# A two-layer decoder trunk on one NeuronCore: products of 258 columns in the short runs of the output projections, and gaps between the later heads' outputs

## The chip, the core and the metric

The kernel runs on one core of one Trainium2 chip. The core has TensorE (PE in the profile; its weight loads are shown apart as PEld), VectorE (DVE), ScalarE (ACT), GpSimd (POOL) and SyncE (SP, which here only starts DMAs). They run side by side and wait for one another through semaphores. The metric is the device time of one execution, in microseconds; lower is better. Three runs of the kernel before gave 556.93, 557.33 and 557.66, median 557.33.

## What is computed

Two layers over 256 tokens of width 1024, in float32. Layer 0 mixes tokens by latent attention, layer 1 by block attention, which at 256 tokens and a block of 256 is causal attention with a relative bias. Each has 8 heads of 128, and each mixer is followed by a squared-ReLU MLP of width 4096.

```python
for i in range(DEPTH):
    h = rms_norm(x, attn_norm[i])
    if i % N_MIXERS == 0:
        x = x + mla_mixer(h, ..., mla_w_o[j], cos, sin)
    else:
        x = x + moba_mixer(h, ..., moba_w_o[j], positions, rel_bias_table)
    h = rms_norm(x, mlp_norm[i])
    x = x + sq_relu_mlp(h, mlp_w_in[i], mlp_w_out[i])
# the last step of either mixer, with out of shape (B, H, S, 128):
out.transpose(0, 2, 1, 3).reshape(B, S, H * 128) @ w_o
```

The change lies in that last step, the output projection, and in one row of layer 1's value projection.

## The kernel before

**Products.** A float32 operand is kept as two parts, a high one rounded to PE's fp32r and the rest as a low one. A product of two such operands is made of three matrix products into the same PSUM bank: high by high, low weight by high activation, high weight by low activation (`mm3`, L87). In most of the program the weights stand still (128 x 128) and the activations move, 256 columns, one for each token. In layer 1's query, key and value rows it is the other way round: the activations of 128 tokens stand still and the weights move, 512 columns in two halves of 256 (`proj1_row`).

**Weights.** They come in units of 128 x 1024 floats. SyncE loads a unit (`load_one`, L158), ScalarE makes the high part (`hi`, L169), VectorE the low part (`lo`, L178). The calls `fill`, `both`, `hi` and `lo` in the program text set where that work stands in each engine's order.

**Order.** The pools are scheduled by hand: every engine runs its instructions in the order in which the program text issues them. So a product that waits holds up all that PE has to do after it.

**Heads.** `run_heads` works through the 8 heads of a layer. For each it issues logits (`A_`), weights of the softmax (`W_`), a transpose (`B_`) and the product with the values (`C_`, `values`, L600 to L606), which leaves the head's output, transposed, as 128 x 256: ScalarE writes the high part into `aT0`, VectorE the low part into `aT1`. Logits, transposes and values are plain float32 on PE. Between them stand short runs of the output projection, in fp32r products:

- `o(h)` adds head h's part to the first four of the eight output blocks; the accumulators `accs` are four PSUM banks. It is 4 x 3 = 12 products. Head 2 is cut into two runs of 6.
- `col(d, heads)` adds heads to one of the last four blocks. Block 4 is taken in pieces: heads 0 and 1 (6 products), 2 and 3 (6), 4 to 6 (9), and 7 (3). Blocks 5 to 7 are taken whole.

Head 6's `o`, the second half of block 4, head 7's `o`, blocks 5 to 7 and the start of the MLP follow each other with no plain float32 product between. That long run has 440 products in the trace, up to the sum of squares inside the MLP (`other_type`).

**Products of 258 columns.** `wider` (L103) makes one of the three products two columns wider than the 256. Its moving operand runs on into the first two columns of whatever lies behind, and its output into two columns of the bank that nobody reads. The third value names which of the three products it is. In the MLP one stands ahead of the first product group after each change of operand kind (the flag `moved`). In `col` there are two: at head 0 and at head 5 of block 4. A bank's columns 256 and 257 have to be written by the first product of the accumulation if a later one adds to them. In layer 1's rows, `proj1_row` with `wide` puts 258 columns in the seventh place and 254 in the last one, so that the row still has its 512; it does so for the first key row and the first query row.

**The heads' outputs.** `aT0` and `aT1` hold 8 x 256 columns each, the heads side by side, so the two columns behind head h are the first two of head h + 1.

Of the kernel before, what the change touches and what calls it, by code (L numbers as in the profile page):

```python
# [11 lines left out]
F32R = mybir.dt.float32r  # L12
# [6 lines left out]
P = 128  # L19


ROOM = {"hT": 416, "aT0": 0, "aT1": 224, "a0": 224, "a1": 224}
D = 1024
S = 256
NT = S // P
KD = D // P
H = 8
# [33 lines left out]
def trunk(ctx: ExitStack, tc: tile.TileContext, A, out):  # L61
    nc = tc.nc
# [8 lines left out]
    def ps():  # L71
        return psum.tile([P, 512], F32, name="ps", tag="ps")
# [14 lines left out]
    def mm3(o, a, b, start, stop, wide=None, between=None):  # L87

        for i, (w, t) in enumerate(((0, 0), (1, 0), (0, 1))):
            if wide and i == wide[2]:  # L90
                mm(wide[0], a[w], wide[1], start and i == 0, stop and i == 2)
            else:
                mm(o, a[w], b[t], start and i == 0, stop and i == 2)
            if between and between[0] == i:
                between[1]()
# [6 lines left out]

    def wider(bank, b, which=0):  # L103
        moved[0] = True
        return bank[:, :S + 2], flat(b[:, :2])[:, :S + 2], which

    def other_type(i, f):
        def run():
# [5 lines left out]
    def flat(ap):  # L114
        return ap.rearrange("p a b -> p (a b)")
# [86 lines left out]
    def part(u, sl):  # L202
        return u[0][:, sl], u[1][:, sl]
# [44 lines left out]
    mhalf = const.tile([P, 32], F32)  # L248
# [295 lines left out]
    def head_tiles(l):  # L544

        cm = ExitStack()
        pool = cm.enter_context(tc.tile_pool(name=f"heads{l}", bufs=1))
        r = []
        for c in range(2):
            r.append({n: pool.tile([P, *sh], F32, name=f"{n}{c}")  # L550
                      for n, sh in (("k", (HG, S)), ("q", (HG, S)), ("v", (NT, HG, P)))})
        room(pool, f"aT{l}")
        aT = [pool.tile([P, H, S], F32R, name=f"aT{i}") for i in range(2)]
        return cm, r, aT

    class Head:


        def __init__(self, hd, aT, h, bias, extra=None):
            self.aT = (aT[0][:, h], aT[1][:, h])  # L560
            self.two = [a[:, h:h + 2] for a in aT] if h < H - 1 else None
            self.i = h % HG
            self.hd = hd[h // HG]
            self.h, self.bias, self.extra = h, bias, extra
# [49 lines left out]
    def out_residual(a, d, gname):  # L614
        nc.vector.tensor_add(x[:, d], a, x[:, d])
        make_h_filled(d, gname)

    def run_heads(hs, proj, post, rows, turn, mid, base, gname, n1):
# [5 lines left out]
        accs = []  # L624

        def o(h, ds=range(4)):
            u = unit(base + h // 2)
            for d in ds:
                if h == 0:
                    accs.append(ps()[:, :S])  # L630
                c = (h % 2) * 512 + d * P
                mm3(accs[d], part(u, slice(c, c + P)), hs[h].aT, h == 0, h == H - 1)
                if h == H - 1:
                    out_residual(accs[d], d, gname)
            if h % 2:
                done(base + h // 2)

# [2 lines left out]
        def col(d, hh):  # L640
            if d not in late:
                late[d] = ps()
            u = unit(base + d)
            for h in hh:

                wide = None
                if d == 4 and h in (0, 5):
                    which = 2 if h and mid is not None else 0
                    wide = wider(late[d], hs[h].two[which // 2], which)
                mm3(late[d][:, :S], part(u, slice(h * P, (h + 1) * P)), hs[h].aT, h == 0, h == H - 1, wide)  # L650
            if hh[-1] == H - 1:
                done(base + d)
                out_residual(late[d][:, :S], d, gname)
# [189 lines left out]
    heads_ctx, hd, aT = head_tiles(0)  # L843
# [56 lines left out]
    post0("k1", 1, on_act=True)  # L900
    fill()

    run_heads([Head(hd, aT, h, bias0, (qpT, kpT)) for h in range(H)], proj0, post0, rows0, turn0, None, O0, "mlp0", 1)
    heads_ctx.close()
    mla_ctx.close()
# [191 lines left out]
    heads_ctx, hd1, aT1 = head_tiles(1)  # L1097
# [3 lines left out]
    def post1(name, t, root=True):  # L1101
        p = open_p.pop((name, t))
        if name[0] == "v":
            nc.scalar.activation(flat(hd1[int(name[1])]["v"][:, t]), p, AF.Copy, scale=r3[0][:, t:t + 1])
        else:
            norms[name, t] = Norm(p, P)
            if root:
                root1(name, t)
# [7 lines left out]
    def turn1(name, t):  # L1116
        tk = slice(t * P, (t + 1) * P)
        to_T(norms[name, t].y, hd1[int(name[1])][name[0]][:, :, tk], gqk[:, 1:2] if name[0] == "q" else None)
# [18 lines left out]

    def proj1(name, t, wide=False):
        open_p[name, t] = ps()
        for _ in proj1_row([(name, t, k, i, half) for k in range(KD) for i in range(3) for half in range(2)], wide):  # L1140
            pass
        if t == NT - 1:
            done(Q0 + 4 * order1[name] + 3)
# [35 lines left out]
    proj1("v0", 1)  # L1179
    fill(2)  # L1180
    post1("v0", 1)
    run_heads([Head(hd1, aT1, h, bias[:, h]) for h in range(H)], proj1, post1, rows1, turn1, lambda: turn1("q0", 1), O1, "mlp1", 2)
    heads_ctx.close()
    mlp(1, M1, [], {}, finish1)
# [74 lines left out]
```

## Time and profile before

| | us |
|---|---|
| runs shown | 556.93, 557.33, 557.66 |
| span of the profiled execution, first to last instruction | 556.0 |
| short runs and what lies between them, layer 0 | 61.0 to 81.6 |
| long run, layer 0 | 81.6 to 131.6 |
| second value row, layer 1 | 333.6 to 339.3 |
| short runs and what lies between them, layer 1 | 347.3 to 365.7 |
| long run, layer 1 | 365.7 to 415.7 |

The span runs from the first to the last instruction of one profiled execution; the time of a run also holds what lies around it, 1.3 us on the median. In rows of the timeline stand the start in us, the length in us, engine, line, operation, output and inputs by the program's names, the shapes, and the number of instructions merged in the row. `ps<-aT,wh` is a product of a head's output with the high part of a weight unit, `ps<-aT,wl` with the low part; `hTh` and `hTl` are the two parts of the normed activations, `pT` and `p` the softmax. In a row of the windows view, each engine's busy time stands with the number of its instructions in the window, then the granted clock, the share of the DMA engines and GB/s. Grouped rows end with count, busy us, mean ns of one, and the idle time before them.

### The profile page before, as it was taken

How to read it: one execution, taken by the hardware profiler on the slowest of the kernel's cores; microseconds unless marked ns; L12 is line 12 of the kernel's file. 1: busy time of each engine (PE TensorE's matmuls, PEld its weight loads, DVE VectorE, ACT ScalarE, POOL GpSimd, SP SyncE). 2: the span in 40 equal slices, each digit the busy share in tenths (PEclk: the TensorE clock that was granted, in tenths of full speed). 3: DMA queues.
4: the chain of work that ended last, by engine and by line, in shares of the span. 5: the costliest groups of instructions: out<-in, count | busy, mean ns of one | idle time of the engine just before them, and what ended most of it. 6: DMA issues, size and time to landing. Idle time of an engine off the chain costs nothing.

```text
span 556.0 us, 11405 instructions
## 1 busy us (share of the span) xinstructions
PE 550.4 (99%) x4648; PEld 538.5 (97%) x4648; DVE 394.4 (71%) x654; ACT 302.5 (54%) x495; POOL 90.6 (16%) x108
## 2 busy tenths in 40 slices
PE   9999999999999999999999999999999999999997
PEld 6888999999999999999999999999999999999997
DVE  5998777688997589965658366777867653977630
ACT  5899675674443364535464465746856432655420
POOL 4692100022132000012232100000130311000100
PEclk9999999999999999999999999999999999999999
DMA  8833534586567366545445554354866764565810
GB/s 294 300 108 128 163 117 152 190 279 191 183 202 220 117 219 195 171 173 186 156 153 195 168 169 145 121 190 121 268 221 184 234 192 148 184 211 175 275 40 28
DMA packets 29188, 99.60 MB, mean 179 GB/s; under 512 B 3824, under 2 KB 4720, under 8 KB 29136
## 3 DMA queue, kind: packets, MB, share of 16 engines
q1 hardware_dynamic: 28656, 97.94, 55.1%
q0 software_dynamic: 336, 0.92, 0.4%
q8 instruction: 36, 0.59, 0.4%
q14 instruction: 16, 0.13, 0.1%
q10 hardware_dynamic: 144, 0.02, 0.0%
HBM read 97.82 MB, written 1.05 MB: 178 GB/s over the span
## 4 chain that ended last, share of the span: by engine, by line
PE 94%; DMA 2%; DVE 1%; SPq 1%; POOL 1%; ACT 1%; issue 0%; ACTq 0%; DVEq 0%
PE ps L85 91%; DMA raw<-in_w_u 2%; PE ps L372 1%; PE ps L596 1%; DMA win<-in_w_in 1%; DVE wl L178 1%; POOL hrs L270 1%; ACT wh L169 0%; SPq L158 0%; PE ps L512 0%; SPq L230 0%; DVE t L352 0%; ACT sqj L477 0%; POOL rs L270 0%; SPq L235 0%
## 5 line engine op out<-in xcount | busy, mean ns | idle before, releaser
L178 DVE TENSOR_TENSOR wl<-raw,wh 128x1024 fp32r<-128x1024 f32 x177 | 218.2, 1249 | 34.9 <-ACT wh L169 34.4
L169 ACT CAST wh<-raw 128x1024 fp32r<-128x1024 f32 x177 | 182.4, 1046 | 69.4 <-PE ps L85 48.7
L85 PE MATMUL ps<-a,wh 128*128 128x256 f32 x1024 | 175.0, 276 | 0.0
L85 PEld LDWEIGHTS ps<-a,wh 128*128 128x128 f32 x1024 | 154.6, 188 | 0.0
L85 PE MATMUL ps<-hTl,wh 128*128 128x256 f32 x512 | 141.9, 277 | 0.0
L85 PE MATMUL ps<-a,wl 128*128 128x256 f32 x512 | 141.9, 277 | 0.0
L85 PE MATMUL ps<-hTh,wl 128*128 128x256 f32 x512 | 141.6, 277 | 0.0
L85 PE MATMUL ps<-hTh,wh 128*128 128x256 f32 x512 | 141.6, 276 | 0.0
L85 PEld LDWEIGHTS ps<-hTh,wh 128*128 128x128 f32 x512 | 96.2, 188 | 0.1
L85 PEld LDWEIGHTS ps<-hTl,wh 128*128 128x128 f32 x512 | 96.2, 188 | 0.1
L85 PEld LDWEIGHTS ps<-a,wl 128*128 128x128 f32 x512 | 96.2, 188 | 0.0
L85 PEld LDWEIGHTS ps<-hTh,wl 128*128 128x128 f32 x512 | 96.2, 188 | 0.0
L940 ACT ACTIVATE t<-ps 128x512 f32<-128x512 f32 (+1 forms) x34 | 19.4, 571 | 62.1 <-PE ps L85 62.1
L85 PE MATMUL ps<-aT,wh 128*128 128x256 f32 (+1 forms) x256 | 50.2, 288 | 0.0
L942 DVE SCALAR_TENSOR_TENSOR t<-ps,t 128x512 f32<-128x512 f32 (+1 forms) x34 | 22.4, 659 | 36.1 <-ACT t L940 35.8
L85 PE MATMUL ps<-wh,hTh 128*128 128x256 f32 (+2 forms) x224 | 45.7, 289 | 0.2 <-ACT wh L169 0.2
L85 PE MATMUL ps<-wh,hTl 128*128 128x256 f32 (+2 forms) x224 | 45.1, 284 | 0.5 <-DVE hTl L280 0.5
L85 PE MATMUL ps<-wl,hTh 128*128 128x256 f32 (+2 forms) x224 | 44.9, 285 | 0.4 <-DVE wl L178 0.3
L85 PEld LDWEIGHTS ps<-aT,wh 128*128 128x128 f32 x256 | 40.3, 188 | 0.2
L85 PE MATMUL ps<-aT,wl 128*128 128x256 f32 x128 | 35.7, 279 | 0.0
L85 PEld LDWEIGHTS ps<-wh,hTh 128*128 128x128 f32 x224 | 34.4, 189 | 1.1 <-issue 0.5
L85 PEld LDWEIGHTS ps<-wh,hTl 128*128 128x128 f32 x224 | 34.7, 188 | 0.8 <-DVE hTl L280 0.8
(167 smaller groups left out, 622.2 us busy)
## 6 DMA issues: line engine op xcount, KB each, us to landing
raw<-in_w_in_mlp SPq DMA_DIRECT2D x64, 512.0 KB, 4.3
raw<-in_w_out_mlp SPq DMA_DIRECT2D x64, 512.0 KB, 4.4
raw<-in_w_qkv SPq DMA_DIRECT2D x24, 512.0 KB, 4.2
raw<-in_w_u SPq DMA_DIRECT2D x8, 512.0 KB, 6.7
win<-in_w_in SPq DMA_DIRECT2D x8, 352.0 KB, 5.1
raw<-in_w_o0a SPq DMA_DIRECT2D x4, 512.0 KB, 3.6
raw<-in_w_o0b SPq DMA_DIRECT2D x4, 512.0 KB, 3.7
raw<-in_w_o1a SPq DMA_DIRECT2D x4, 512.0 KB, 4.2
```

Of the source, the lines that this page charges most:

```text
L85: nc.tensor.matmul(o, a, b, start=start, stop=stop)
L169: (eng.copy if eng is nc.scalar else eng.tensor_copy)(his[i][:, :w], raws[i][:, :w])
L178: eng.tensor_sub(los[i][:, :w], raws[i][:, :w], f32(his[i][:, :w]))
L270: nc.gpsimd.tensor_tensor(dst, t, mhalf[:, :n].rearrange("p (a b) -> p a b", b=t.shape[-1]) if len(t.shape) == 3 else mhalf[:, :n], op=OP.pow)
L372: nc.tensor.transpose(pt[:, i * P:(i + 1) * P], yf[:, i * P:(i + 1) * P], ident)
L596: nc.tensor.transpose(pt[:, i * P:(i + 1) * P], self.p[:, i * P:(i + 1) * P], ident)
L940: nc.scalar.activation(rl, src, AF.Relu)
L942: nc.vector.scalar_tensor_tensor(sq, src, 0.0, rl, op0=OP.max, op1=OP.mult)
```

## The change

- The heads' outputs get a new layout: flat, with 64 floats (256 bytes) between heads 4 and 5, 5 and 6, and 6 and 7. Heads 0 to 4 stay side by side. `fill_gaps` writes the first two columns of each gap, in both parts: one copy on GpSimd for `aT0` and one for `aT1`, ahead of `run_heads` in each layer.
- `o(h)`: head 0 takes 258 columns in the first product of output blocks 0, 1 and 2; heads 1, 2, 4, 5 and 6 in the third product of the first block of a run, so head 2 twice. Heads 3 and 7 stay as they are.
- `col(4, ...)`: head 2 takes 258 columns in its third product, beside heads 0 and 5 as before.
- Layer 1's second value row gets the 258 and the 254 that the first key row and the first query row have.

```diff
--- before.py
+++ after.py
@@ -19,6 +19,7 @@
 P = 128
 
 
+GAP = 64
 ROOM = {"hT": 416, "aT0": 0, "aT1": 224, "a0": 224, "a1": 224}
 D = 1024
 S = 256
@@ -102,7 +103,7 @@
 
     def wider(bank, b, which=0):
         moved[0] = True
-        return bank[:, :S + 2], flat(b[:, :2])[:, :S + 2], which
+        return bank[:, :S + 2], (b if len(b.shape) == 2 else flat(b[:, :2]))[:, :S + 2], which
 
     def other_type(i, f):
         def run():
@@ -550,15 +551,22 @@
             r.append({n: pool.tile([P, *sh], F32, name=f"{n}{c}")
                       for n, sh in (("k", (HG, S)), ("q", (HG, S)), ("v", (NT, HG, P)))})
         room(pool, f"aT{l}")
-        aT = [pool.tile([P, H, S], F32R, name=f"aT{i}") for i in range(2)]
+        aT = [pool.tile([P, H * S + 3 * GAP], F32R, name=f"aT{i}") for i in range(2)]
         return cm, r, aT
 
+    def fill_gaps(aT):
+
+        for a in aT:
+            nc.gpsimd.tensor_copy(a[:, 5 * S:].rearrange("p (a b) -> p a b", b=GAP + S)[:, :, :2],
+                                  mhalf[:, :6].rearrange("p (a b) -> p a b", b=2))
+
     class Head:
 
 
         def __init__(self, hd, aT, h, bias, extra=None):
-            self.aT = (aT[0][:, h], aT[1][:, h])
-            self.two = [a[:, h:h + 2] for a in aT] if h < H - 1 else None
+            c = h * S + max(h - 4, 0) * GAP
+            self.aT = (aT[0][:, c:c + S], aT[1][:, c:c + S])
+            self.two = [a[:, c:c + S + 2] for a in aT] if h < H - 1 else None
             self.i = h % HG
             self.hd = hd[h // HG]
             self.h, self.bias, self.extra = h, bias, extra
@@ -627,11 +635,16 @@
             u = unit(base + h // 2)
             for d in ds:
                 if h == 0:
-                    accs.append(ps()[:, :S])
+                    accs.append(ps())
                 c = (h % 2) * 512 + d * P
-                mm3(accs[d], part(u, slice(c, c + P)), hs[h].aT, h == 0, h == H - 1)
+                wide = None
+                if h == 0 and d < 3:
+                    wide = wider(accs[d], hs[h].two[0])
+                elif h not in (0, 3, H - 1) and d == ds[0]:
+                    wide = wider(accs[d], hs[h].two[1], 2)
+                mm3(accs[d][:, :S], part(u, slice(c, c + P)), hs[h].aT, h == 0, h == H - 1, wide)
                 if h == H - 1:
-                    out_residual(accs[d], d, gname)
+                    out_residual(accs[d][:, :S], d, gname)
             if h % 2:
                 done(base + h // 2)
 
@@ -644,8 +657,8 @@
             for h in hh:
 
                 wide = None
-                if d == 4 and h in (0, 5):
-                    which = 2 if h and mid is not None else 0
+                if d == 4 and h in (0, 2, 5):
+                    which = 2 if h == 2 or h and mid is not None else 0
                     wide = wider(late[d], hs[h].two[which // 2], which)
                 mm3(late[d][:, :S], part(u, slice(h * P, (h + 1) * P)), hs[h].aT, h == 0, h == H - 1, wide)
             if hh[-1] == H - 1:
@@ -900,6 +913,7 @@
     post0("k1", 1, on_act=True)
     fill()
 
+    fill_gaps(aT)
     run_heads([Head(hd, aT, h, bias0, (qpT, kpT)) for h in range(H)], proj0, post0, rows0, turn0, None, O0, "mlp0", 1)
     heads_ctx.close()
     mla_ctx.close()
@@ -1137,6 +1151,7 @@
 
     def proj1(name, t, wide=False):
         open_p[name, t] = ps()
+        wide = wide or (name, t) == ("v1", 1)
         for _ in proj1_row([(name, t, k, i, half) for k in range(KD) for i in range(3) for half in range(2)], wide):
             pass
         if t == NT - 1:
@@ -1179,6 +1194,7 @@
     proj1("v0", 1)
     fill(2)
     post1("v0", 1)
+    fill_gaps(aT1)
     run_heads([Head(hd1, aT1, h, bias[:, h]) for h in range(H)], proj1, post1, rows1, turn1, lambda: turn1("q0", 1), O1, "mlp1", 2)
     heads_ctx.close()
     mlp(1, M1, [], {}, finish1)
```

What PE has in its order for the head-0 and head-1 runs of layer 0 (`aT_477` is the high part, `aT_478` the low part; in brackets the engines that an instruction waits for). First the second half of head 0 and the first block of head 1 before:

```order
L85 MATMUL ps<-aT_477,wh 128x256
L85 MATMUL ps<-aT_477,wl 128x256
L85 MATMUL ps<-aT_478,wh 128x256
L85 MATMUL ps<-aT_477,wh 128x256 [waits PE_49]
L85 MATMUL ps<-aT_477,wl 128x256
L85 MATMUL ps<-aT_478,wh 128x256
L372 MATMUL ps<-ident,t_906 128x128 [waits DVE_49]
L372 MATMUL ps<-ident,t_906 128x128 x3
L85 MATMUL ps<-pT,v_473 128x256 [waits Activation_49]
L85 MATMUL ps<-pT,v_473 128x128
L85 MATMUL ps<-aT_477,wh 128x256
L85 MATMUL ps<-aT_477,wl 128x256
```

And the same place of the change, beginning four rows further on:

```order
L86 MATMUL ps<-aT_477,wl 128x256
L86 MATMUL ps<-aT_478,wh 128x256
L373 MATMUL ps<-ident,t_908 128x128 [waits DVE_49]
L373 MATMUL ps<-ident,t_908 128x128 x3
L86 MATMUL ps<-pT,v_473 128x256 [waits Activation_49]
L86 MATMUL ps<-pT,v_473 128x128
L86 MATMUL ps<-aT_477,wh 128x256
L86 MATMUL ps<-aT_477,wl 128x256
L86 MATMUL ps<-aT_478,wh 128x258 [waits DVE_49]
L86 MATMUL ps<-aT_477,wh 128x256
```

No product has changed its place; the third one of head 1 has two columns more and a wait for VectorE, which writes head 2's low part. On POOL, what stands ahead of the heads of layer 0 in the change:

```order
L271 TENSOR_TENSOR hrs<-hss,mhalf 128x4 [waits DVE_49] x4
L560 CAST aT_477<-mhalf 128x3x2 [waits DMAHW4_49,DMAHW5_49,DMAHW3_49,DMAHW7_49,DMAHW2_49,DMAHW0_49]
L560 CAST aT_478<-mhalf 128x3x2
L271 TENSOR_TENSOR hrs<-hss,mhalf 128x4 [waits DVE_49,Pool_49] x2
L302 TENSOR_TENSOR ssum<-t_1515,t_1588 128x512 [waits Activation_49]
```

The two copies are new; they stand between the square roots of the key rows and those of the last query rows. The wait is for DMAs into memory that `aT0` and `aT1` take over.

## The prediction

> **What bounds the kernel now.** I read the page first: busy times, the granted clock and the chain that ended last.
>
> ```profile
> span 556.0 us, 11405 instructions
> PE 550.4 (99%) x4648; PEld 538.5 (97%) x4648; DVE 394.4 (71%) x654; ACT 302.5 (54%) x495; POOL 90.6 (16%) x108
> PEclk9999999999999999999999999999999999999999
> PE 94%; DMA 2%; DVE 1%; SPq 1%; POOL 1%; ACT 1%; issue 0%; ACTq 0%; DVEq 0%
> ```
>
> TensorE is busy for 99% of the span at an undivided clock, and 94% of the chain are its own instructions. So what a product costs is its pitch, the time from its start to the next one's start, and a pitch that shrinks anywhere on PE shortens the span unless a later wait swallows it. "Took" in the rows (276 to 280 ns) is longer than the pitch because products overlap; pitches have to be read from start times.
>
> The second view is the timeline of PE. The first two rows below are from one of the short runs (head 5 on the first four output blocks, layer 0), the next two from the first MLP product. Rows alternate over the three partial products, so two rows of the same tiles lie a multiple of three products apart.
>
> ```profile
> 79.74 0.28 PE L85 MATMUL ps<-aT,wl 128*128 128x256 f32 x1
> ...
> 80.80 0.28 PE L85 MATMUL ps<-aT,wl 128*128 128x256 f32 x1
> 114.97 0.28 PE L85 MATMUL ps<-hTl,wh 128*128 128x256 f32 x1
> ...
> 117.01 0.28 PE L85 MATMUL ps<-hTl,wh 128*128 128x256 f32 x1
> 84.00:131.00 47.00, 47.00 (x417) 47.00 (x416) 34.80 (x48) 29.70 (x43) 7.36 (x7) 1.00 0.63 204
> L85 PE MATMUL ps<-aT,wl 128*128 128x256 f32 x33 | 9.2, 280 | 0.0
> L85 PE MATMUL ps<-aT,wl 128*128 128x256 f32 x30 | 8.3, 276 | 0.0
> ```
>
> The first pair is 9 products apart: 1.06 / 9 = 117.8 ns. The second is 18 apart: 2.04 / 18 = 113.3 ns. The windows row says that it holds for long: 47 us with 417 products, of which two or three only reach into the window, so again 113.3 ns. Same shape, same clock, two pitches: **slow 117.7 and fast 113.3, a difference of 4.4 ns**. The last two rows group the low-part products by form, from 61 to 83.4 us and from 84 to 131 us: a mean of 280 ns, nearly all slow, and of 276, all fast. The shown length differs as the pitch does, so either number tells them apart.
>
> The third reading is what turns one into the other. These rows are the end of one query row of layer 1 and the start of the next, with 254 and 258 columns in them.
>
> ```profile
> 282.79 0.39 PE L85 MATMUL ps<-wl,hTh 128*128 128x256 f32 x2
> 283.01 0.28 PE L85 MATMUL ps<-wh,hTl 128*128 128x254 f32 x1
> 283.13 0.40 PE L85 MATMUL ps<-wh,hTh 128*128 128x256 f32 x2
> 283.37 0.40 PE L85 MATMUL ps<-wh,hTl 128*128 128x256 f32 x2
> 283.60 0.40 PE L85 MATMUL ps<-wl,hTh 128*128 128x256 f32 x2
> 283.84 0.28 PE L85 MATMUL ps<-wh,hTl 128*128 128x258 f32 x1
> 283.96 0.40 PE L85 MATMUL ps<-wh,hTh 128*128 128x256 f32 x2
> 284.19 0.39 PE L85 MATMUL ps<-wh,hTl 128*128 128x256 f32 x2
> 284.42 0.28 PE L85 MATMUL ps<-wl,hTh 128*128 128x256 f32 x1
> ```
>
> Two products take 0.22 before the one of 254 and 0.24 behind it: it ended the fast pitch. Behind the one of 258, two more take 0.23 to 0.24, and then 0.23 for two: it began it. Everywhere that a 258 stands at the fifth product of a run or later, the pitch falls to fast two products behind it and stays. Every change of operand kind (transposes, logits, values between the runs) puts it back to slow: of the short output runs all start slow but one (layer 0, at 75.37). Those runs are 6 or 12 products long and end before anything makes them fast. That is the stretch that the change touches.
>
> **The change part by part.** *The short runs.* I count a wide product at place w (from 1) as making place w+2 the first fast one, as above. No run of before has one at the third place; it lies between the fifth, where it always works, and the first, where it didn't (the second rival), nearer to the fifth in that the run is under way, so I take it to work, and nothing gained is the other end. Runs of 12 with the wide product third (heads 1, 4, 5): 8 fast products each. Runs of 6 (head 2 twice; heads 2 and 3 of block 4): 2 each, but none in layer 0 for the last, which is the run that starts fast already. Head 0, with wide products at 1, 4 and 7: I count from the fourth, 7. Head 3 gets none. Head 6 opens the long run that goes on into block 4; there the fast pitch so far comes with the 258 at the head-5 product of block 4, the 16th of the run in layer 0 and the 18th in layer 1, and will come 13 and 15 products earlier. Layer 0: 3 x 8 + 2 x 2 + 7 + 13 = 48. Layer 1: 3 x 8 + 3 x 2 + 7 + 15 = 52. A hundred products at 4.4 ns: 0.44 us.
>
> *The second value row of layer 1.* It is the one row of its kind that never gets fast by itself:
>
> ```profile
> 333.87 0.40 PE L85 MATMUL ps<-wh,hTl 128*128 128x256 f32 x2
> ...
> 339.05 0.40 PE L85 MATMUL ps<-wl,hTh 128*128 128x256 f32 x2
> 326.56 0.39 PE L85 MATMUL ps<-wl,hTh 128*128 128x256 f32 x2
> 326.79 0.39 PE L85 MATMUL ps<-wh,hTh 128*128 128x256 f32 x2
> ```
>
> From the first to the second row 44 products take 5.18 us, 117.7 each; the row before it, of the same shape, was at 0.23 for two by its fifth product. With the wide product seventh, 40 of 48 become fast: 0.18 us.
>
> *What it adds.* Twenty wide products, ten a layer, besides the one of the value row, whose 254 takes its two columns back. Two columns of 256 at 117.7 ns are 0.9 ns; 20 of them 0.02 us. Whether a column costs that or nothing cannot be told apart here.
>
> *The added waits.* A wide product reads two columns of the next head's output, so head 1's waits for the low half of head 2, and the first of head 2 for that of head 3, which VectorE writes; those of heads 4 to 6 read the gap, which POOL fills.
>
> ```profile
> 62.12 0.42 DVE L606 TENSOR_TENSOR aT<-ps,aT 128x256 fp32r<-128x256 f32 x1
> 64.21 0.42 DVE L606 TENSOR_TENSOR aT<-ps,aT 128x256 fp32r<-128x256 f32 x1
> 63.85 0.40 PE L85 MATMUL ps<-aT,wh 128*128 128x256 f32 x2
> 65.70 0.40 PE L85 MATMUL ps<-aT,wh 128*128 128x256 f32 x2
> 58.02 1.01 POOL L270 TENSOR_TENSOR hrs<-hss,mhalf 128x4 f32<-128x4 f32 x1 [9.85 <-DVE hss L359]
> 320.47 1.01 POOL L270 TENSOR_TENSOR hrs<-hss,mhalf 128x4 f32<-128x4 f32 x1 [4.06 <-DVE hss L347]
> ```
>
> The two halves are ready at 62.54 and 64.63; the products that now need them start at 63.85 and 65.70, 1.3 and 1.1 us later. PE is some 0.1 us earlier there, so the waits cost nothing; had they been late, everything on PE would stand behind them. The four copies on POOL stand in front of these square roots, after 9.85 and 4.06 us of idle time. No row shows such a copy; between nothing and the 1.01 us of the root each, two are at most 2.0 us, inside both gaps. Cover gone, the root, the row and PE would be late by the rest; I take nothing. The first copy also waits for loads into memory used at the start, long landed by then.
>
> *What swallows part of it.* One PE wait lies among the runs:
>
> ```profile
> 356.79 0.47 PE L85 MATMUL ps<-aT,wh 128*128 128x258 f32 x1
> PEld ps L85 <- DVE wl L178: 0.3, 1, 0.3
> ```
>
> PE stands 0.3 us until VectorE has made the low part of a weight unit. VectorE's work ahead of it follows PE's logits, so what PE gains before those comes through; what it gains between them (2 products, 0.01 us) does not. Sum: 0.44 + 0.18 - 0.02 - 0.01 = **0.59 us** off the profiled execution, whose span is 556.0; the median of the runs shown is 557.33, 1.3 us more, and I let that stand: 557.33 - 0.59 = 556.74, said as **556.8**. There is a ceiling: layer 0 has 12 + 12 + 6 + 6 + 12 + 6 + 12 + 12 + 17 = 95 slow products, layer 1 103, the value row 48. All of them fast would be 246 x 4.4 = 1.08 us, just under the 0.2% (1.11 us) that a measurement of this kernel can tell from no change.
>
> The Trainium skill, in "TensorE: Matmul & The Clock Gate", section "Back-to-back issue gap", gives a warm product of N columns N / 2.4 + 2.5 ns. By it 256 columns have one pitch, 109 ns, and 258 only add 0.8. Both pitches above lie over it and differ at one N, so the trace disagrees here.
>
> **The rivals.** *A second wide product undoes the first.* No run of before has a 258 at the fast pitch, and the change makes several: the later ones of head 0, and above all the head-5 product of block 4, which follows head 6's. The 254 above ended the fast pitch at once; if a shift of two columns against some period of four is what counts, two shifts of 258 end it too. Then what is left of the long runs (440 - 16 = 424 products in layer 0, 422 in layer 1) goes slow until the next change of kind: 846 x 4.4 = 3.72 us. Of the 0.59 gained, head 0's 0.03 go too: 557.33 + 3.72 - 0.56 = 560.5, slower. Against it: a product of 254 also starts eight bytes off, so that may have done it, and the fast pitch lasts through thousands of products while other engines' work changes beside it. It decides at the first 258 among fast products. If it happens in one layer only: 557.33 + 1.87 - 0.59 = 558.6.
>
> *Near a run's start the wide product doesn't hold.* In the only run that has one at its first place without a stall, this is seen:
>
> ```profile
> 72.37 0.47 PE L85 MATMUL ps<-aT,wh 128*128 128x258 f32 x1
> 72.68 0.28 PE L85 MATMUL ps<-aT,wl 128*128 128x256 f32 x1
> 72.79 0.40 PE L85 MATMUL ps<-aT,wh 128*128 128x256 f32 x2
> 73.03 0.28 PE L85 MATMUL ps<-aT,wl 128*128 128x256 f32 x1
> 73.15 0.28 PE L85 MATMUL ps<-aT,wh 128*128 128x256 f32 x1
> ```
>
> One pitch of 0.11, then 0.24 for two and 0.12: fast once, then slow. If all short runs do so, the long run's 28 products and the value row's 40 remain: 0.30 us, 557.0. Against it: at the fifth place or later none fell back.
>
> *Width has no part in it* (chance, or the row's operands, sets the pitch). Then nothing is gained and 0.02 us lost: 557.35. The rows around 283 speak against it. By the rule of the Trainium skill above the time would be the same 557.35.
>
> **How the numbers follow.** Forecast 0.58 (own range 556.3 to 557.3); undone in both long runs 0.20, in one 0.05; not holding near the start 0.12; width without effect 0.05. The range takes the forecast, the two rivals without change and the one-layer case, and leaves out the 0.20: 556.1 to 558.7. Slower by over 0.2%: 0.25. Faster by over 0.2% lies above the ceiling and needs the scatter of the runs, 0.05. Within: 0.70.
>
> **What would show it.** Right: rows of 12 in which the pitch falls from 117.7 to 113.3 two products behind the 258, a mean of about 277 ns for the aT products, the value row 0.18 us shorter, and 113.3 behind both 258s of the long run. Wrong by the first rival: 117.7 and a shown 280 ns over 84 to 131 us and 370 to 415 us. Wrong by a wait: idle time of PE behind VectorE or POOL at a 258. A 258 behind which the pitch stays at 117.7, or a run that now starts at another pitch, breaks the count of products.

## The result, and the profile after

The change makes the kernel slower. Its median is 560.86 us (five runs, 560.65 to 561.31) against 557.51 for the kernel before beside it (five runs, 556.93 to 557.67): a ratio of 1.0065, with a 95% interval from 1.0055 to 1.0076. The forecast was 556.8, in a range up to 558.7.

The page of the changed kernel, with the span, the busy times and the chain that ended last:

```profile
span 559.5 us, 11410 instructions
PE 554.2 (99%) x4648; PEld 542.3 (97%) x4648; DVE 394.1 (70%) x654; ACT 302.3 (54%) x495; POOL 92.7 (17%) x112
PE 96%; POOL 2%; DMA 1%; SPq 1%; issue 0%; DVE 0%
```

The span grew by 3.5 us and PE's busy time by 3.8, with the same 4648 matmuls. PE is as full as before and the chain is PE's own to a still higher share. So no new wait took the time; the same products take longer. The windows view of PE shows where (window, its length, PE busy with the number of its products, then clock, DMA share and GB/s), over the stretches in the two long runs that the prediction named. The third row is the second window in the kernel before. Behind it stand two grouped rows of the changed kernel by form: low-part MLP products from 370 to 415 us, and low-part head products in the short runs of layer 0, from 61 to 81 us. Line L85 of the kernel before is L86 in the changed one. A product of 258 columns is called a 258.

```profile
84.00:131.00 47.00, 47.00 (x402) 1.00 0.66 204
370.00:415.00 45.00, 45.00 (x385) 1.00 0.64 198
370.00:415.00 45.00, 45.00 (x399) 1.00 0.64 199
L86 PE MATMUL ps<-hTl,wh 128*128 128x256 f32 x99 | 27.6, 279 | 0.0
L86 PE MATMUL ps<-aT,wl 128*128 128x256 f32 x28 | 7.8, 279 | 0.0
```

In the same 47 us stood 417 products before; now there are 402, and the clock is still 1.00. With the two or three that reach in, 402 in 47 us are 117.6 ns each. Layer 1 has 385 products where 399 stood, and the fourth row says the same: 279 ns shown, the slow length. The fifth row is the disappointment on the other side: the short runs, which the change was to make fast, still show 279 ns.

The timeline gives the place where each long run turns. The first two rows are the start of layer 0's run and of the sum of squares behind it in the kernel before; the others are the changed kernel:

```profile
81.60 0.36 PE L85 MATMUL ps<-aT,wh 128*128 128x256 f32 x1
131.63 0.38 PE L85 MATMUL ps<-ssum,ones 128*128 128x256 f32 x1
81.46 0.36 PE L86 MATMUL ps<-aT,wh 128*128 128x256 f32 x1
...
81.78 0.40 PE L86 MATMUL ps<-aT,wh 128*128 128x258 f32 x2
82.02 0.28 PE L86 MATMUL ps<-aT,wl 128*128 128x256 f32 x1
82.13 0.39 PE L86 MATMUL ps<-aT,wh 128*128 128x256 f32 x2
...
83.15 0.39 PE L86 MATMUL ps<-aT,wh 128*128 128x256 f32 x2
83.38 0.28 PE L86 MATMUL ps<-aT,wl 128*128 128x256 f32 x1
83.50 0.40 PE L86 MATMUL ps<-aT,wh 128*128 128x256 f32 x2
...
133.32 0.59 PE L86 MATMUL ps<-ssum,ones 128*128 128x256 f32 x2
```

The row at 81.78 begins with head 6's 258. It and the product behind it take 0.24 us, and then the pitch is fast: the nine products from 82.13 to 83.15 take 1.02 us, 113.3 ns each. The second of the pair at 83.15 is the 258 at head 5 of block 4. From there on the pitch is slow, for the run's last 424 products, to the sum of squares at 133.32. The run took 131.63 - 81.60 = 50.03 us before and takes 133.32 - 81.46 = 51.86 now: +1.83. Layer 1's does the same behind 13 fast products, with 422 products at the slow pitch, and went from 365.66 to 415.70 (50.04) to 367.35 to 419.19 (51.84): +1.80.

The two long runs are 3.63 us of the 3.5. The rest nets out: the first long run starts 0.14 earlier than before (0.17 was there at 53.4 us already, ahead of every edit on PE), the value row lost 0.18, and the query row behind it (`q1`, first 128 tokens), which was slow in the trace before, happened to be fast in this one, some 0.2.

The value row itself, layer 1:

```profile
328.02 0.39 PE L86 MATMUL ps<-wh,hTl 128*128 128x256 f32 x2
328.25 0.39 PE L86 MATMUL ps<-wl,hTh 128*128 128x256 f32 x2
328.48 0.28 PE L86 MATMUL ps<-wh,hTl 128*128 128x258 f32 x1
328.59 0.40 PE L86 MATMUL ps<-wh,hTh 128*128 128x256 f32 x2
328.82 0.40 PE L86 MATMUL ps<-wh,hTl 128*128 128x256 f32 x2
329.06 0.40 PE L86 MATMUL ps<-wl,hTh 128*128 128x256 f32 x2
```

It begins fast, 0.23 for two, and the 258 ends that: 0.23 and 0.24 alternate to the row's end. This row starts at 327.70 after and at 326.01 before. There it was fast by itself; the prediction, and the table of times ahead of it, took the query row at 333.87 for it.

### The profile page after: what moved, and what is told of

It is laid out like the page before. It is cut to its first block, busy times and chain, and to the rows that moved or that the text cites. A ratio compares the mean times of both kernels' runs of the same rounds, so it can differ in the third digit from the quotient of the medians.

```text
span 559.5 us, 11410 instructions
## 1 busy us (share of the span) xinstructions
PE 554.2 (99%) x4648; PEld 542.3 (97%) x4648; DVE 394.1 (70%) x654; ACT 302.3 (54%) x495; POOL 92.7 (17%) x112
## 4 chain that ended last, share of the span: by engine, by line
PE 96%; POOL 2%; DMA 1%; SPq 1%; issue 0%; DVE 0%
PE ps L86 93%; PE ps L373 1%; PE ps L604 1%; DMA rowp<-in_rowp 1%; POOL rr L412 0%; SPq L159 0%; POOL gsc L426 0%; SPq L231 0%; POOL ang L394 0%; POOL pr L411 0%; PE ps L513 0%; POOL rr L416 0%; POOL posf L392 0%; DVE t L1087 0%; POOL kk L403 0%
## 5 line engine op out<-in xcount | busy, mean ns | idle before, releaser
L86 PE MATMUL ps<-a,wh 128*128 128x256 f32 x1024 | 175.0, 276 | 0.0
L86 PEld LDWEIGHTS ps<-a,wh 128*128 128x128 f32 x1024 | 154.5, 188 | 0.0
L86 PE MATMUL ps<-hTl,wh 128*128 128x256 f32 x512 | 142.5, 278 | 0.0
L86 PE MATMUL ps<-hTh,wl 128*128 128x256 f32 x512 | 142.2, 278 | 0.0
L86 PE MATMUL ps<-hTh,wh 128*128 128x256 f32 x512 | 142.0, 277 | 0.0
L86 PE MATMUL ps<-a,wl 128*128 128x256 f32 x512 | 141.7, 277 | 0.0
L86 PEld LDWEIGHTS ps<-hTh,wl 128*128 128x128 f32 x512 | 96.1, 188 | 0.0
L86 PEld LDWEIGHTS ps<-a,wl 128*128 128x128 f32 x512 | 96.1, 188 | 0.0
L86 PEld LDWEIGHTS ps<-hTh,wh 128*128 128x128 f32 x512 | 96.1, 188 | 0.1
L86 PEld LDWEIGHTS ps<-hTl,wh 128*128 128x128 f32 x512 | 96.0, 188 | 0.1
L86 PE MATMUL ps<-aT,wh 128*128 128x256 f32 (+1 forms) x256 | 51.0, 289 | 0.0
L86 PE MATMUL ps<-wh,hTl 128*128 128x256 f32 (+2 forms) x224 | 45.3, 284 | 0.5 <-DVE hTl L281 0.5
L86 PE MATMUL ps<-wh,hTh 128*128 128x256 f32 (+2 forms) x224 | 45.7, 289 | 0.0
L86 PE MATMUL ps<-wl,hTh 128*128 128x256 f32 (+2 forms) x224 | 45.0, 285 | 0.3 <-DVE wl L179 0.3
L86 PEld LDWEIGHTS ps<-aT,wh 128*128 128x128 f32 x256 | 40.5, 188 | 0.2
L86 PE MATMUL ps<-aT,wl 128*128 128x256 f32 x128 | 35.8, 280 | 0.0
L86 PEld LDWEIGHTS ps<-wh,hTl 128*128 128x128 f32 x224 | 34.7, 188 | 0.8 <-DVE hTl L281 0.8
L86 PEld LDWEIGHTS ps<-wl,hTh 128*128 128x128 f32 x224 | 34.5, 188 | 0.9 <-DVE wl L179 0.8
```

Source lines behind the costliest of these rows:

```text
L86: nc.tensor.matmul(o, a, b, start=start, stop=stop)
```

## The experiments

Pitches below are read from start times in the traces; "slow" and "fast" are said of products, 117.8 and 113.3 ns. The letters in the expectations are those of each experiment's own theories.

### e1: the second 258 of the long run taken out

The first theory was the prediction's rival: the 258 at head 5 of block 4 meets the fast pitch and ends it. Without it, head 6's should hold to the end.

```diff
--- after.py
+++ e1.py
@@ -657,7 +657,7 @@
-                if d == 4 and h in (0, 2, 5):
+                if d == 4 and h in (0, 2):
```

> The changed kernel without the 258 at head 5 of block 4; head 6's own 258 stays. Theory A (the second 258 in a run that is already at 113 ns per product brings it back to 118): the 424 and 422 products behind it are at 113.3 again, 3.7 us less than the changed kernel, 557.1; the long runs show 113.3 from head 6's 258 on. Rival B (the new layout of the heads' outputs, or anything else of the change, holds the MLP at 118): still 560.9, 118 in both long runs.

Measured: 557.04 us (10 runs) against 557.24 (25 runs), ratio 0.9997, 0.9987 to 1.0007. One edit of two columns, made once in each layer, takes back the whole loss. PE's windows in e1:

```profile
84.00:131.00 47.00, 47.00 (x417) 1.00 0.64 204
370.00:415.00 45.00, 45.00 (x399) 1.00 0.63 201
```

Head 6's 258 makes 436 products fast in either layer, the first of them two places behind it, as the prediction had counted. That the 28 products which the long runs thereby win (0.12 us) don't show is no surprise: it is below what the interval can tell. The value row began slow this time, for five products, and its 258 made it fast. The same edit at the same place ended a fast row in the changed kernel and began one here.

### e2: also without the 258 of the value row

```diff
--- e1.py
+++ e2.py
@@ -1151,7 +1151,6 @@
     def proj1(name, t, wide=False):
         open_p[name, t] = ps()
-        wide = wide or (name, t) == ("v1", 1)
```

> As the run before it in this list, and layer 1's second value row without its 258 and 254. Theory A: that row is fast by itself from its second or third product on, as in the kernel before, so its 40 products are back at 113.3: 0.18 us less than without this edit, 556.9 to 557.0. Rival (the 258 of that row was neutral and the row slow for another reason): the row stays at 118, no difference.

Measured: 557.09 (10 runs), ratio 0.9999, 0.9990 to 1.0008. The value row was fast by itself, and the query row behind it slow for 47 products, as in the trace before. Between e1 and e2 the value row's edit costs or saves nothing that shows; its price in the changed kernel, 0.18 us, rests on the trace alone.

### e3: the layout and the gap copies without any new 258

```diff
--- after.py
+++ e3.py
@@ -635,13 +635,8 @@
                 wide = None
-                if h == 0 and d < 3:
-                    wide = wider(accs[d], hs[h].two[0])
-                elif h not in (0, 3, H - 1) and d == ds[0]:
-                    wide = wider(accs[d], hs[h].two[1], 2)
...
-                if d == 4 and h in (0, 2, 5):
-                    which = 2 if h == 2 or h and mid is not None else 0
+                if d == 4 and h in (0, 5):
+                    which = 2 if h and mid is not None else 0
...
-        wide = wide or (name, t) == ("v1", 1)
```

> The kernel before with the new layout and the four copies on GpSimd, and none of the new 258s. Theory A (the layout costs nothing): 557.5, the same pitches as before in every run of products. Rival B (the layout sets the pitch, because the low parts and heads 5 to 7 lie 256 bytes off): long runs or short runs change their pitch; 560 or more if the long runs do.

Measured: 557.28 (10 runs), ratio 1.0003, 0.9993 to 1.0012. The 256 bytes between the outputs and the four copies cost nothing that shows, and both long runs turn fast at head 5's 258, as before. The value row was slow throughout in this trace and the query row behind it fast: which of them is slow changes with the kernel, although neither was touched here.

### e4: sixteen wide products in one unbroken run

e1 shows that a second 258 can undo the first, but not by what rule. Rivals: the pitch toggles at each 258; or the added columns count modulo some period, so that one group in every so many is fast; or 258s act and other widths do not; or a second 258 matters in the heads' runs alone. Layer 1's second MLP product has two times eight groups of 48 products, with nothing of another kind between the groups. Each group got a wide product at its start, three of the last eight one with more columns.

```diff
--- before.py
+++ e4.py
@@ -106,0 +107,9 @@
+    MORE = {(1, 0): [2] * 8, (1, 1): [2, 4, 2, 8, 2, 16, 2, 2]}
+
+    def more(bank, b, l, r, d):
+        if not moved[0]:
+            return wider(bank, b)
+        if (l, r) in MORE:
+            n = S + MORE[l, r][d]
+            return bank[:, :n], flat(b[:, :2])[:, :n], 0
...
-                            wider(bank, a[0]) if f == 0 and not moved[0] else None,
+                            more(bank, a[0], l, r, d) if f == 0 else None,
```

> The kernel before with one wide product at the start of each of the 16 output groups of 48 products in layer 1's MLP, 258 columns in all but three, which have 260, 264 and 272 (fourth to last first: groups 10, 12 and 14). All 48 products of a group then show one pitch. Theory A1 (each 258 turns the pitch over): groups alternate 118, 113, 118, ...: of the first nine groups five slow, four fast, about 1.9 us in all sixteen and the stretch between the two halves. Theory A2 (columns count modulo some period above four): one fast group in every so many, the period read from the distance of the fast ones; up to 5 us slower. Theory A3 (a 258 ends the fast pitch and another of them nearly always brings it back, but other widths do not matter): as A1 up to group 9, then no change at 260, 264 and 272. Theory C (the second 258 matters in the heads' runs alone): all groups at 113, same time.

Measured: 561.89 us (one run), 4.65 over the kernel before. PE's windows, the same 5 us behind the wide product of each of the first seven groups:

```profile
421.90:426.90 5.00, 5.00 (x45) 1.00 0.38 115
427.55:432.55 5.00, 5.00 (x45) 1.00 0.70 235
433.20:438.20 5.00, 5.00 (x47) 1.00 0.88 290
438.65:443.65 5.00, 5.00 (x45) 1.00 0.70 201
444.30:449.30 5.00, 5.00 (x45) 1.00 0.71 195
449.95:454.95 5.00, 5.00 (x47) 1.00 0.68 206
455.40:460.40 5.00, 5.00 (x45) 1.00 0.69 198
```

PE was at the fast pitch ahead of the first group. That group's 258 ended it, the second left the run slow, the third brought the fast pitch back, the fourth ended it, and so on: one group in three is fast. Not two, so it is no toggle, and not four. From start times, groups at the slow pitch have a mean of 117.76 to 117.79 ns, groups at the fast pitch 113.33. Away from a 258 the slow mean is made of single pitches of 117 to 119 ns, and any three in a row come to 353 or 354 ns, 353.3 in the mean.

The four ways in which a 258 acted can be told from the pitches that follow it: 114, 119, 120, 117 where it ended the fast pitch; 118, 120, 113, 118 where one product is fast and then none; 119, 117, 114, 113 where it brings it; and 119, 120, 121, 118 where nothing comes of it, seen three times behind the wider products of the second piece. Those products of 260, 264 and 272 columns stand at one place each and settle nothing about the width. Whether 258s must be counted, or the distance between them, e4 leaves open: all of them stand 48 apart, a multiple of three.

### e5 and e6: the short runs' 258 at the fourth and at the fifth product

If a place in a cycle of three counts, heads 1, 2, 4 and 5, whose 258 at the third product of their run did nothing that lasted, should answer at another. Both kernels are e2 (head 6's 258 stays third, head 5's in block 4 stays out) with the place changed; head 0 is wide on all four blocks.

```diff
--- e2.py
+++ e5.py
@@ -22,0 +23 @@
+PLACE = {(6, 0): 2}
@@ -641,5 +642,6 @@
-                if h == 0 and d < 3:
+                at = PLACE.get((h, ds[0]), 3)
+                if h == 0:
                     wide = wider(accs[d], hs[h].two[0])
-                elif h not in (0, 3, H - 1) and d == ds[0]:
-                    wide = wider(accs[d], hs[h].two[1], 2)
+                elif h not in (3, H - 1) and d == ds[0] + at // 3:
+                    wide = wider(accs[d], hs[h].two[at % 3 // 2], at % 3)
--- e5.py
+++ e6.py
@@ -642 +642 @@
-                at = PLACE.get((h, ds[0]), 3)
+                at = PLACE.get((h, ds[0]), 4)
```

> The changed kernel without the 258 at head 5 of block 4 and without those of the value row, and with the 258 of heads 1, 2, 4 and 5 at the fourth product of each run instead of the third (head 6 keeps the third; head 0 has one at the start of all four blocks). Theory A (the products at 118 ns go through a cycle of three places, and a 258 brings 113 at one of the three only): the third place brought 113 in none of these runs, so either the fourth or the fifth does; where it is the fourth, the run of 12 has 7 products at 113. Theory B (a short run cannot become fast so near its start): all stay at 118. Both: the long runs at 113, 557.0 as far as one run can tell.

> As the run before it in this list, with the 258 at the fifth product of those runs. Theory A: the runs that stayed at 118 with the third and the fourth place now turn, with 6 products at 113 in a run of 12; those that turned with the fourth do not. Theory B: all stay at 118.

Measured: 566.13 us for e5 and 557.65 for e6, beside 557.26 (one run each). In e5 PE's windows in both long runs and in layer 1's MLP are slow:

```profile
84.00:131.00 47.00, 47.00 (x401) 1.00 0.63 202
370.00:415.00 45.00, 45.00 (x385) 1.00 0.62 198
430.00:470.00 40.00, 40.00 (x342) 1.00 0.67 208
```

In e5 the long run of layer 0 began fast by itself, and head 6's 258, the very one that begins the fast pitch in the changed kernel and in e1, ended it. In layer 1 it had no lasting effect, one fast product and then none; and behind it the 258 at the fifth product of the MLP, untouched and effective before, had no more, for 1198 products. So 423 and 421 more slow products in the long runs and 1198 in the MLP: 2042 x 4.44 ns = 9.1 us, of the 8.9 measured. What had changed ahead of them is the 258's place, by one product, in some short runs, and a fourth wide product at head 0. The start of a run therefore depends on what went before it, and head 6's place is lucky, not safe. Whether e5 comes out so in every execution, one run can't tell; e1's ten all lie between 556.51 and 557.43.

The short runs themselves: of the six of 12 products (heads 1, 4 and 5), three turned fast with the 258 at the fourth product (heads 4 and 5 of layer 0, head 1 of layer 1) and three with it at the fifth (head 4 of both layers, head 5 of layer 1); only head 1 of layer 0 did so at neither. So both expectations held in part: short runs can turn, but e5's time was 9 us off, and in e6 head 4 of layer 0 turned once more, where it was expected not to, and head 1 of layer 0 not at all. Head 0's wide products, three apart, never worked, with three of them or with four. e6's 0.4 us over the run beside it is less than single runs of the kernel before differ by (556.72 to 557.69 in e1's 25); 0.2 of it are the value row, which was slow by itself in that trace.

### e7: two 258s at distances of 5 to 20 products

This separates counting from distance. In each group of layer 1's second MLP product one 258 stands first and another 5, 6, 7 ... 20 products behind it.

```diff
--- before.py
+++ e7.py
@@ -106,0 +107,9 @@
+    def more(bank, a, l, r, d, f):
+        if l == 0:
+            return wider(bank, a[0]) if f == 0 and not moved[0] else None
+        m = 5 + 8 * r + d
+        if f == 0:
+            return wider(bank, a[0])
+        if f == m // 3:
+            return wider(bank, a[m % 3 // 2][:, f:f + 2], m % 3)
...
-                            wider(bank, a[0]) if f == 0 and not moved[0] else None,
+                            more(bank, a, l, r, d, f),
```

> The kernel before with two products of 258 columns in each of the 16 output groups of 48 in layer 1's MLP: the first product of the group, and another one 5, 6, 7, ... 20 products behind it, one distance per group. Theory A (a cycle of three places): where the group's first 258 ended the fast pitch, the second one brings it back at one distance of every three, 5, 8, 11, ... or 6, 9, 12, ... or 7, 10, 13, ...; in the run with 258 at every group's start, which is 48 apart and so a multiple of three, it took two more. Theory B (the number of 258s alone counts, three to the round): a second one never brings it back by itself and the fast pitch comes after every third 258, whatever the distance. Time by A or B: between 2 and 5 us above the kernel before.

Measured: 559.52 us (one run). In the third group a 258 had ended the fast pitch; the next, 7 products behind it, brings it back:

```profile
433.77 0.28 PE L85 MATMUL ps<-a,wl 128*128 128x258 f32 x1
433.89 0.39 PE L85 MATMUL ps<-a,wh 128*128 128x256 f32 x2
434.12 0.28 PE L85 MATMUL ps<-a,wl 128*128 128x256 f32 x1
434.23 0.39 PE L85 MATMUL ps<-a,wh 128*128 128x256 f32 x2
```

In the fourth the distance is 8, and nothing comes of it:

```profile
439.37 0.40 PE L85 MATMUL ps<-a,wh 128*128 128x258 f32 x2
439.60 0.28 PE L85 MATMUL ps<-a,wl 128*128 128x256 f32 x1
439.73 0.40 PE L85 MATMUL ps<-a,wh 128*128 128x256 f32 x2
439.96 0.28 PE L85 MATMUL ps<-a,wl 128*128 128x256 f32 x1
440.08 0.40 PE L85 MATMUL ps<-a,wh 128*128 128x256 f32 x2
```

Three products take 0.34 us in the first (433.89 to 434.23) and 0.35 in the second (439.73 to 440.08), and so on to the next group's 258.

From a 258 that ended the fast pitch, the next one brought it back at distances 7, 10, 13, 16 and 19 (five of five), and not at 5, 8, 11, 14, 17 and 20 (none of six). After these failures the next group's 258, 48 products behind the one that ended it, gave one fast product; from that one, distances 6, 9, 12, 15 and 18 brought it back. So it is the distance modulo three. A rule fits all of e7 and e4's first eight groups: slow products run through a cycle of three places. A 258 one place past the ending one makes the run fast; at the same place as the ending one it shifts the cycle by a place, so that the next at a multiple of three works; at the third place it does nothing.

The short runs bear this out in part. Head 5 of layer 0 and heads 4 and 5 of layer 1, taken over the changed kernel, e5 and e6, show the three effects at their third, fourth and fifth products in the order of the rule; the other three runs do not. And behind head 0's 258s of the changed kernel, layer 0, the pitches are 119, 120, 121 at the fourth product and 119, 117, 118 at the seventh, where by the rule a 258 three products behind one without effect should repeat it. So the rule is shown for unbroken runs, not for the first products of a run.

### e8 and e9: the rule put to the test in the long run

Both are the changed kernel without the value row's edit, with head 5's 258 (the one that ends the fast pitch) at the first product of its three, and a third 258 behind it: four products in e8, five in e9. By the rule the first must restore the fast pitch in both layers and the second must not.

```diff
--- after.py
+++ e8.py
@@ -657,8 +657,8 @@
-                if d == 4 and h in (0, 2, 5):
-                    which = 2 if h == 2 or h and mid is not None else 0
+                if d == 4 and h in (0, 2, 5, 6):
+                    which = {0: 0, 2: 2, 5: 0, 6: 1}[h]
...
-        wide = wide or (name, t) == ("v1", 1)
--- e8.py
+++ e9.py
@@ -661 +661 @@
-                    which = {0: 0, 2: 2, 5: 0, 6: 1}[h]
+                    which = {0: 0, 2: 2, 5: 0, 6: 2}[h]
```

> The changed kernel without the value row's edit, and with a third 258 in the long run: head 6's own at the third product of the run, head 5's of block 4 (its first product in both layers), and a new one four products behind that, at head 6 of block 4. Theory A (from a 258 that ended the fast pitch on, products go through a cycle of three places, and a 258 brings 113 back at a distance of 1, 4, 7, ... products from it): head 5's ends the fast pitch, the new one brings it back, both long runs are at 113.3 from there on, 557.1. Theory B (any second 258 ends it and only every third one counts, at whatever distance): stays at 118, 560.8.

> As the run before it in this list, with the new 258 one product later, five behind head 5's. Theory A: five is not 1 modulo 3, so both long runs stay at 118 for 419 and 419 products, 3.7 us more: 560.8. Theory C (any further 258 turns the pitch over again): 557.1, as at a distance of four.

Measured: e8 557.44 us (10 runs), ratio 0.9998, 0.9988 to 1.0007; e9 560.97 (4 runs), ratio 1.0059, 1.0042 to 1.0076; the kernel before beside both 557.53 (13 runs). The timeline of e8 at its third 258, layer 0, and its window of the long run:

```profile
83.75 0.28 PE L86 MATMUL ps<-aT,wl 128*128 128x258 f32 x1
83.86 0.39 PE L86 MATMUL ps<-aT,wh 128*128 128x256 f32 x2
84.09 0.28 PE L86 MATMUL ps<-aT,wl 128*128 128x256 f32 x1
...
84.00:131.00 47.00, 47.00 (x417) 1.00 0.66 205
```

The same of e9, whose third 258 is the first of the pair at 83.52:

```profile
83.52 0.40 PE L86 MATMUL ps<-aT,wh 128*128 128x258 f32 x2
83.76 0.28 PE L86 MATMUL ps<-aT,wl 128*128 128x256 f32 x1
83.88 0.40 PE L86 MATMUL ps<-aT,wh 128*128 128x256 f32 x2
84.12 0.28 PE L86 MATMUL ps<-aT,wl 128*128 128x256 f32 x1
...
84.00:131.00 47.00, 47.00 (x402) 1.00 0.64 202
```

The two products behind e8's take 0.23 us (83.86 to 84.09), the two behind e9's 0.24 (83.88 to 84.12), and so it goes on: 417 products in the window against 402, and 419 at one pitch or the other in each layer. One product's place of one 258 is worth 3.5 us of 560. None of e1, e2 and e8 is measurably better than the kernel before; the ceiling of 1.08 us, in which all of the slow head products and the value row would have to turn, is itself at the edge of what can be told.

## Why the prediction was wrong, point by point

**The step that failed** is the count of what a 258 does: "I count a wide product at place w (from 1) as making place w+2 the first fast one, as above." It treats a 258 as something that only ever adds fast products. The rows around 283 us showed one 258 among slow products, and the text went from there to "everywhere that a 258 stands at the fifth product of a run or later". That 258 stands seven products behind the 254 that had ended the fast pitch, one of the distances at which e7's 258s brought it back; whether a 254 sets the cycle as a 258 does was not tried. The runs showed that what it does depends on the pitch it meets and, among slow products, on its place in a cycle of three (e4, e7, and tested forward in e8 and e9). Among fast products it ends the fast pitch: in every group of e4 and e7 that began fast, in both long runs of the changed kernel, and in all 21 places of the eleven traces where a 258 has three fast products just ahead of it. The prediction's sum had no term for this; in the two long runs it measured 3.63 us.

**The long runs.** The prediction did see where this would be decided, "at the first 258 among fast products", and the price: 846 products, 3.72 us, and 560.5 for the time. The numbers were right: 424 and 422 slow products, less the 24 that had become fast ahead of them, are 822 x 4.44 ns = 3.65 us; 3.63 was measured in the two runs. It had 0.20 as its chance, because the only case seen was a product of 254 that also started eight bytes off. That product's share is still not separated from its width; it was not needed, since 258 alone does it (e1). In that rival's sum head 0's share is 14 products in two layers, 0.06 and not 0.03, which leaves its time at 560.5.

**The short runs.** Counted at 24 + 4 + 7 products in layer 0 and 24 + 6 + 7 in layer 1; measured, none that lasted. In head 2's second run of either layer the fifth product shows 113 and 114 ns, as counted, and the run ends with the sixth; head 2's run of block 4 in layer 1 began fast by itself, and its 258 ended that. Head 6's place worked: its fast pitch came at the fifth product of the long run and lasted for 11 and 13 products, to the second 258; with e1 all of the 13 and 15 products counted for it (0.12 us) came. The rival of "near a run's start the wide product doesn't hold" had the outcome for these runs, but its reason falls: a run's third product was late enough for head 6, and at the fourth and fifth three runs each turned fast while three did not (e5, e6).

**The value row.** The term of 0.18 us had the wrong row: the rows at 333.87 to 339.05 are a query row (`q1`, first 128 tokens). The value row begins at 326.01 and the rows quoted as "the row before it" are its own. So the edit met a fast row, and cost 40 products, 0.18 us in the trace, where it was to save as much. The order of PE's instructions around 326 would have shown it. Even rightly named it had no sure sign: the row began slow in e1 and in e3. Nor does every change of operand kind put the pitch back to slow, as the prediction read it: this row follows a transpose and is fast behind its first three products in the trace before.

**What was put at nothing shows nothing.** The layout and the copies: e3, 1.0003. The copies themselves, which no row could show before, are in POOL's timeline of the changed kernel, two in a row in each layer:

```profile
47.96 0.33 POOL L560 CAST aT<-mhalf 128x6 fp32r<-128x6 f32 x2
57.85 1.01 POOL L271 TENSOR_TENSOR hrs<-hss,mhalf 128x4 f32<-128x4 f32 x1 [9.56 <-DVE hss L360]
301.36 0.49 POOL L560 CAST aT<-mhalf 128x6 fp32r<-128x6 f32 x2
```

0.33 and 0.49 us, within the bounds of 0 to 2.0, with 9.56 us of idle time left behind the first pair. The second pair stands ahead of the root at 316.25, with 14.40 us left behind it, and not ahead of the one that the prediction named (320.47 before, 322.16 after, 4.06 us of idle time in both). The added waits: PE's view of its waits (line, what it waited for, us in total, times, longest) has the same three for VectorE, of the same lengths, as that of the kernel before, and none at a 258 that the change added:

```profile
PE ps L86 <- DVE warm L219: 1.0, 1, 1.0
PE ps L86 <- DVE hTl L281: 0.5, 1, 0.5
PE ps L86 <- DVE wl L179: 0.3, 1, 0.3
```

**Width without effect** had 0.05 and is excluded by e8 against e9, where 258 columns at one place or the next decide 838 products.

## What to carry to other kernels

An effect seen at one place of a program ("this odd size makes what follows faster") is an edge between two conditions until a second one in a row has been tried: ask first what the edit does where its effect is already there, and price that case over everything that lies behind it. Where a small edit sets the pitch of hundreds of instructions, a gain of tenths of a microsecond ahead of them has to be weighed against all of them. And where a term rests on rows of a timeline, name the row from the order of the engine's instructions, not from its look.

## What the runs showed of the hardware

- One shape of product at one granted clock, 1.00, has two lasting pitches: 113.33 ns, and 117.77 ns in the mean with three products at 353.3 ns (e4). In the long runs and in layer 1's MLP either lasted for all of the hundreds of products behind it until a product of another width or a change of kind. In layer 1's query, key and value rows the pitch also turned fast with no 258, within the first eight products (the row at 319.01 in the trace before), and the row at 295.33 of that trace was slow for four products behind a pitch of 388 ns. The Trainium skill, in "TensorE: Matmul & The Clock Gate", section "Back-to-back issue gap", gives the gap of an isolated warm product of N columns as N / 2.4 + 2.5 ns, one value for each width. By it the change would have cost twenty times 0.8 ns, an estimate of 0.02 us, and the runs show 3.35 us.
- A product two columns wider ends the fast pitch at once (21 of 21), and in an unbroken run brings it back at one of three places of the slow one (e7: 5 of 5 at distances of one more than a multiple of three, 0 of 6 at two more; e8 and e9 foretold by it).
- The place at which a run of products starts in this cycle depends on what PE did before it: the same 258 at the third product of layer 0's long run made 436 products fast in e1 and ended the fast pitch in e5. By the rule a 258 takes each of the four conditions (fast, or slow at one of three places) to a different one or leaves it, and no two to the same. So no fixed row of them could make a run fast from every start. That is argued from the rule, which is not shown for the first products of a run, and was not tried.
- What in the chip has a cycle of three is open. The three partial products of `mm3` also come in threes, in an order that the experiments did not change, and a kernel with two or four in turn was not tried.
